# Two-layer hybrid encoder trunk on one core: the projections' [tokens, columns] copies turned by VectorE squares and tile-to-tile DMAs instead of TensorE transposes

## The chip, the core and the metric

The kernel runs on one core of a Trainium2 chip. The metric is the device time of one execution in microseconds, as a median of repeated runs. The profile comes from one execution of the same program under the hardware profiler.

## What is computed

The reference runs two layers of a mixer over 256 tokens of width 2048 in float32. Cut to what matters:

```python
h = rmsnorm(x, pre_norm_g[l])
proj = jnp.einsum('bsd,dn->bsn', h, w_in[l])
(qa, ka, va, qb, kb, vb, qc, kc, vc, za, zb, zc, gates) = jnp.split(proj, split_points, axis=-1)
ya = neighbourhood_attention(heads(qa, 8), heads(ka, 8), heads(va, 8), rpb[l])
yb = gqa_attention(axial_rope(rmsnorm(qb)), axial_rope(rmsnorm(kb)), vb)
yc = dilated_mixture(heads(qc, 12), heads(kc, 12), heads(vc, 12))
merged = sum(g_i * einsum(y_i * silu(z_i), w_branch_i) for the branches a, b, c)
x = x + rmsnorm(einsum(merged, w_out[l]), post_norm_g[l])
```

The scores need q and k with the head's 128 columns on the partitions and tokens along the free axis, and the branch products need silu(z) times the attention output in the same layout. The projections leave PSUM with tokens on the partitions. Turning them from [tokens, columns] to [columns, tokens] is the work this case is about.

## The kernel before

All weights stream once through the core. The unit is a chunk: 256 rows by 512 columns of a weight matrix (512 KB, tile `raw`). ScalarE casts it to a rounded high part `wh` (L171), VectorE subtracts to get the low part `wl` (L176), and TensorE multiplies both token tiles T = 0, 1 (128 tokens each) with it in three passes per 128 rows (high by high, low by high, high by low; L146 to L148). That is 12 matmuls of 512 columns a chunk. A projection block (512 output columns) has 8 chunks; a layer has 23 projection blocks for q, k, v and z, then four rounds of gates and branch products, then four output blocks.

The order is written out by hand and each engine runs its own list in order. For each chunk `ahead` issues the load of the chunk 6 later on SyncE's queue (SP), the cast of the chunk 3 later and the subtraction of the chunk 2 later; after the chunk's matmuls `slot()` adds a little of the other work. `slot()` takes up to two steps of the evacuation queue `evq`, one step of every job that has started (`active`), and then starts one waiting job: a light one from `light`, once its slot has passed, or, if `light` is empty, an attention head from `heavy`.

An evacuation of a q, k or z block copies PSUM to the tile `tok` (ScalarE, L299 or L325, the z blocks with a VectorE step at L326; the branch B blocks with the rotation at L483 to L493), first for T = 0 and a slot later for T = 1. Each then calls `later(tr_job(...))`. `tr_job` (L280) is the code that changes. For one token tile it makes four TensorE transposes against the identity into the PSUM tile `tp` (L284), and then either splits `tp` into a high part (ScalarE, L130) and a low part (VectorE, L132), or, for the operands that are used unsplit, copies it (ScalarE, L289). A layer has 17 blocks of four 128-column heads and one (the keys of branch B) of two, so 36 blocks in the program and 280 transposes. Of the 18 blocks of a layer 9 are split (q and k of branch A and of group 0 of branch C, q and k of branch B) and 9 are copied (five z blocks, q and k of groups 1 and 2 of branch C).

Nearly every tile lives in one pool `up` of 47 buffers of 4 KB a partition (helper `U`): weights before and after the split, `tok`, the attention operands and the probabilities. A load waits on SP until the buffer that it gets has been released.

The attention jobs (`head_job`, `job_c`) also use TensorE transposes, of the probabilities (L140, L380). These stay.

Of the kernel before, what the change touches and what calls it, by code (L numbers as in the profile page):

```python
# [10 lines left out]
F32 = mybir.dt.float32  # L11
# [9 lines left out]
P = 128  # L21
# [6 lines left out]
LA_RAW, LA_HI, LA_LO = 6, 3, 2  # L28
LAG = 6


class Blk:
    """One 512-column block of a projection: K chunks of 256 rows, both token tiles."""

# [13 lines left out]
def trunk(ctx, tc, x, xT, wpack, wbr_a, wbr_b, wbr_c, wout, pre_g, qk_g, bgate, post_g, abias,  # L48
# [31 lines left out]
    nc.gpsimd.memset(mhalf, -0.5)  # L80
    # the engines wake while the first loads are under way
    nc.scalar.activation(mhalf[:, 0:1], mhalf[:, 0:1], AF.Copy)
# [5 lines left out]

# [1 line left out]
    evq, light, heavy, active = deque(), deque(), deque(), []  # L90
    flow = dict(cool=0, hold=True, slot=0, split=9)

    def later(g, wait=0):
        """a filler for a following slot, once what it needs is under way"""
        light.append((flow["slot"] + wait, g))
# [24 lines left out]

# [1 line left out]
    def rsqrt(v, n):  # L122
        """1/sqrt of a small positive f32 tile"""
        y = small.tile([P, n], F32, name="rs_y")
        nc.gpsimd.tensor_tensor(out=y, in0=v, in1=mhalf[:, :n], op=ALU.pow)
        return y

    def split(src, h, lo, scale=1.0):
        """src * scale -> h + lo, both exactly representable for the one-pass products."""
        nc.scalar.activation(h, src, AF.Copy, scale=scale)  # L130
        if isinstance(scale, float) and scale == 1.0:
            nc.vector.tensor_tensor(out=lo, in0=src, in1=f32(h), op=ALU.subtract)  # L132
        else:
            nc.vector.scalar_tensor_tensor(lo, src, scale, f32(h), op0=ALU.mult, op1=ALU.subtract)

    def four_T(src):
        """Four [128,128] transposes side by side in one bank."""
        tp = aux.tile([P, 4, P], F32, name="tp", bufs=2)
        for j in range(4):
            nc.tensor.transpose(tp[:, j, :], src(j), ident)  # L140
        return tp

    def mm3(out_, lhs, rhs, first, last):
        """out_ += lhs.T @ rhs for (high, low) pairs: one-pass products"""
        (lh, ll), (rh, rl) = lhs, rhs
        nc.tensor.matmul(out_, lhsT=lh, rhs=rh, start=first, stop=False)  # L146
        nc.tensor.matmul(out_, lhsT=lh, rhs=rl, start=False, stop=False)  # L147
        nc.tensor.matmul(out_, lhsT=ll, rhs=rh, start=False, stop=last)  # L148

# [1 line left out]
    stream = []  # L151
# [51 lines left out]

# [1 line left out]
    prev = {}  # L205

    def layer(l):
# [5 lines left out]

        # -- the layer's input: hT = (x * gain) transposed, 1/rms kept apart --
        def sq_step(nb, T):
# [23 lines left out]
        def ht_x(nb, js):  # L239
            """from the host's transposed layout of x"""  # L240
            t = S["xT", nb]
            if nb not in HT:
                HT[nb] = pair("hT", [4, 256])
            for j in js:
                split(t[:, j], HT[nb][0][:, j], HT[nb][1][:, j], scale=gain(nb * 4 + j))

        def ht_psum(nb, T):
            """from the previous layer's output: residual, transposes"""
            if nb not in HT:
                HT[nb] = pair("hT", [4, 256])  # L250
            h, lo = HT[nb]
            tp = four_T(lambda j: X[nb][:, T, j * P:(j + 1) * P])
            c = slice(T * P, (T + 1) * P)
            t = work.tile([P, 4, P], F32, name="s", bufs=2)
            g = gpre[:, l * 16 + nb * 4:l * 16 + nb * 4 + 4]
            for j in range(4):
                nc.scalar.activation(t[:, j], tp[:, j], AF.Copy, scale=g[:, j:j + 1])
            split(t, h[:, :, c], lo[:, :, c])
# [19 lines left out]

        # -- evacuations, per token tile --
        def tr_job(dst, tok, T, n=4):  # L280
            """token-major [tok, n x 128] -> dst[column, block, tokens of T]; a pair is split"""
            tp = aux.tile([P, 4, P], F32, name="tp", bufs=2)
            for j in range(n):
                nc.tensor.transpose(tp[:, j, :], tok[:, T, j * P:(j + 1) * P], ident)  # L284
            c = slice(T * P, (T + 1) * P)
            if isinstance(dst, tuple):
                split(tp[:, 0:n], dst[0][:, 0:n, c], dst[1][:, 0:n, c])
            else:
                nc.scalar.copy(dst[:, 0:n, c], tp[:, 0:n])  # L289
            yield  # L290

        def evac_qk(store, key, which, two):
            tok = {}

            def f(T, ps):
                if T == 0:
                    tok[0] = U("tok", [2, 512])
                    store[key] = pair("qk", [4, 256]) if two else U("qkT", [4, 256])
                nc.scalar.activation(tok[0][:, T], ps, AF.Copy, scale=S[which][T])  # L299
                later(tr_job(store[key], tok[0], T))  # L300
                yield
            return f
# [14 lines left out]
        def evac_z(key):  # L317
            tok = {}

            def f(T, ps):  # L320
                if T == 0:
                    tok[0] = U("tok", [2, 512])
                    SZ[key] = U("z", [4, 256])
                z = tok[0][:, T]
                nc.scalar.activation(z, ps, AF.Tanh, scale=S["rsh"][T])  # L325
                nc.vector.scalar_tensor_tensor(z, z, 1.0, ps, op0=ALU.add, op1=ALU.mult)  # L326
                later(tr_job(SZ[key], tok[0], T), 1)
                yield
            return f

        # -- attention --
        def softmax(sc, p, n, w, f=None):
            """n x w logits a row: exp(f * (s - max)), and the sums"""
            nm = small.tile([P, n], F32, name="nm")
# [10 lines left out]
        def norm(p, sm, n, rsh):  # L345
            """rows divided by their sums, times the gate's factor of the token"""
            r = small.tile([P, n], F32, name="rsum")
# [12 lines left out]
        def head_job(zb, hh, q, k, v, bias=None, f=None):  # L360
            """one head over all 256 keys, both token tiles: q, k give (high, low) of [d, tokens],
            v those of [keys of a tile, d]"""
            sc = aux.tile([P, 2, 256], F32, name="sc")
# [43 lines left out]
        def job_c(hh, dist):  # L407
            """one merged head: the three groups' keys under one softmax"""
            q, k = [QT["c", g] for g in range(3)], [KT["c", g] for g in range(3)]
# [39 lines left out]

        # -- branch A: two units of four heads --  # L450
        def a_unit(u):
# [15 lines left out]

        # -- branch B --
        def b_tables():
# [9 lines left out]
        def rope(dst, ps, T, n, which):  # L479
            """dst = rotation of ps (n heads), the norm's gain in the tables; in two steps"""  # L480
            tb = S["rope"]
# [14 lines left out]
        def head_norm(ps, T, n):  # L496
            """1/rms of each head (of the normalised input's projection)"""
            ss = small.tile([P, n], F32, name="hss")
# [7 lines left out]
        def evac_qb(u):  # L506
            tok = {}

            def f(T, ps):
# [6 lines left out]
                nc.vector.tensor_scalar(S["bf", u][:, :, T], y, S["rss"][T], None, op0=ALU.mult)  # L516
                later(tr_job(QT["b", u], tok[0], T), 1)
                if T == 1:
                    for hh in range(4):
                        heavy.append((2, job_b(u, hh)))  # L520
            return f

        def evac_kvb(T, ps):
# [11 lines left out]
            for i in range(2):  # L535
                t = tok[:, T, i * P:(i + 1) * P]
                nc.scalar.activation(t, t, AF.Copy, scale=f[:, i:i + 1])
            later(tr_job(KT["b"], tok, T, n=2), 1)

# [5 lines left out]

        # -- gates and branch products --
        def merge(nb):
# [44 lines left out]

        # -- output projection, post norm, residual --
        OG, PG, R3 = {}, {}, {}
# [40 lines left out]

        # -- the order of the layer's blocks --
        first = proj(22, evac_z(("c", 0)))
# [56 lines left out]

# [1 line left out]
    nc.sync.dma_start(out=gpre, in_=pre_g)  # L696
# [60 lines left out]
def _tokens():  # L757
    """[2, 128]: the tokens of each tile, t = 4 i + 2 T + s at row 64 s + i"""
    T, s, i = np.meshgrid(np.arange(2), np.arange(2), np.arange(64), indexing="ij")
    return (4 * i + 2 * T + s).reshape(2, P)  # L760
# [27 lines left out]
def _bias_index():  # L788
    """[2, 128, 256] indices into a head's flat (15 x 31) table, 465 where masked"""
    tok = _tokens()  # L790
# [9 lines left out]
def _pack(w):  # L800
    """[L, K, N] -> [L, N/512, K/256, 128, 2*512]"""
    L, K, N = w.shape
# [49 lines left out]
```

## Time and profile before

| | |
|---|---|
| median of 3 runs | 2075.34 us (2074.78 to 2075.48) |
| profiled execution, first to last instruction (span) | 2073.5 us; no other time of that execution is listed |
| TensorE (PE) busy | 2061.9 us, 99% of the span |
| VectorE (DVE) busy | 1163.2 us, 56% |
| ScalarE (ACT) busy | 951.4 us, 46% |
| mean granted TensorE clock | 0.999 |
| bytes moved by DMA | 397.81 MB, 192 GB/s over the span |

PE stands for TensorE's matmuls, PEld for its weight loads, SPq for the issuing of DMAs on SyncE's queue. Matmuls overlap in the pipeline: a matmul is shown with 390 ns, but one starts every 0.23 us, so what an instruction costs on PE is read from the distance between starts, not from its duration.

### The profile page before, as it was taken

How to read it: one execution, taken by the hardware profiler on the slowest of the kernel's cores; microseconds unless marked ns; L12 is line 12 of the kernel's file. 1: busy time of each engine (PE TensorE's matmuls, PEld its weight loads, DVE VectorE, ACT ScalarE, POOL GpSimd, SP SyncE). 2: the span in 40 equal slices, each digit the busy share in tenths (PEclk: the TensorE clock that was granted, in tenths of full speed). 3: DMA queues.
4: the chain of work that ended last, by engine and by line, in shares of the span. 5: the costliest groups of instructions: out<-in, count | busy, mean ns of one | idle time of the engine just before them, and what ended most of it. 6: DMA issues, size and time to landing. Idle time of an engine off the chain costs nothing.

```text
span 2073.5 us, 24944 instructions
## 1 busy us (share of the span) xinstructions
PE 2061.9 (99%) x9634; PEld 1716.2 (83%) x9634; DVE 1163.2 (56%) x1445; ACT 951.4 (46%) x1370; POOL 23.2 (1%) x31
## 2 busy tenths in 40 slices
PE   9999999999999999999999999999999999999998
PEld 7888888888888888888888888888888888888886
DVE  6444466565776554645554445565657764646454
ACT  6443354444554434443564444454445543443332
POOL 0000000000000000000000000000000000000000
PEclk9999999999999999999999999999999999999999
DMA  9555455645546655667565554555454466656662
GB/s 373 190 173 187 153 173 179 213 156 185 168 163 208 203 198 188 203 228 259 174 228 171 188 183 142 182 176 200 164 187 163 168 213 200 197 191 208 228 241 71
DMA packets 115270, 397.81 MB, mean 192 GB/s; under 512 B 12752, under 2 KB 12880, under 8 KB 115152
## 3 DMA queue, kind: packets, MB, share of 16 engines
q1 hardware_dynamic: 115152, 396.23, 56.5%
q8 instruction: 75, 1.23, 0.2%
q14 instruction: 43, 0.35, 0.1%
HBM read 391.99 MB, written 4.19 MB: 191 GB/s over the span
## 4 chain that ended last, share of the span: by engine, by line
PE 99%; DMA 0%; ACT 0%; DVE 0%; SPq 0%; issue 0%; DVEq 0%; POOLq 0%; ACTq 0%
PE acc L148 31%; PE acc L146 31%; PE acc L147 31%; PE tp L284 1%; PE tp L140 1%; PE tp L380 1%; PE o L148 0%; PE sc L148 0%; PE o L147 0%; PE sc L147 0%; PE o L146 0%; PE sc L146 0%; DMA raw<-in_wpack_dram 0%; PE o L446 0%; PE sc L418 0%; DVE x L597 0%
## 5 line engine op out<-in xcount | busy, mean ns | idle before, releaser
L176 DVE TENSOR_TENSOR wl<-raw,wh 128x1024 fp32r<-128x1024 f32 (+1 forms) x706 | 831.7, 1217 | 172.1 <-ACT wh L171 169.3
L146 PE MATMUL acc<-wh,hTh 128*128 128x512 f32 x2240 | 886.3, 396 | 0.6 <-ACT wh L171 0.6
L147 PE MATMUL acc<-wl,hTh 128*128 128x512 f32 x2240 | 873.8, 390 | 0.8 <-DVE wl L176 0.8
L148 PE MATMUL acc<-wh,hTl 128*128 128x512 f32 x2240 | 873.8, 390 | 0.0
L171 ACT CAST wh<-raw 128x1024 fp32r<-128x1024 f32 (+1 forms) x706 | 699.3, 1043 | 40.0 <-DVE wl L176 12.9
L148 PEld LDWEIGHTS acc<-wh,hTl 128*128 128x128 f32 x2240 | 420.6, 188 | 89.0
L147 PEld LDWEIGHTS acc<-wl,hTh 128*128 128x128 f32 x2240 | 421.5, 188 | 84.9 <-DVE wl L176 2.6
L146 PEld LDWEIGHTS acc<-wh,hTh 128*128 128x128 f32 x2240 | 421.2, 188 | 83.3 <-ACT wh L171 1.6
L564 ACT ACTIVATE g<-g 128x512 f32<-128x512 f32 x48 | 30.4, 633 | 232.8 <-DVE g L563 232.8
L563 DVE SCALAR_TENSOR_TENSOR g<-acc,rsx,bg 128x512 f32<-128x512 f32 x48 | 35.9, 747 | 173.6 <-PE acc L148 173.6
L146 PE MATMUL acc<-wh,yTh 128*128 128x512 f32 x320 | 124.5, 389 | 0.0
L147 PE MATMUL acc<-wl,yTh 128*128 128x512 f32 x320 | 124.5, 389 | 0.0
L148 PE MATMUL acc<-wh,yTl 128*128 128x512 f32 x320 | 124.5, 389 | 0.0
L146 PE MATMUL acc<-wh,mTh 128*128 128x512 f32 x256 | 100.4, 392 | 0.0
L148 PE MATMUL acc<-wh,mTl 128*128 128x512 f32 x256 | 99.7, 390 | 0.0
L147 PE MATMUL acc<-wl,mTh 128*128 128x512 f32 x256 | 99.7, 389 | 0.0
L299 ACT ACTIVATE tok<-acc,rsx 128x512 f32<-128x512 f32 x40 | 27.6, 689 | 124.9 <-PE acc L148 124.9
L340 ACT ACTIVATE sp<-sp,nm 128x256 f32<-128x256 f32 (+1 forms) x48 | 27.6, 577 | 109.4 <-DVE nm L335 109.4
L579 DVE SCALAR_TENSOR_TENSOR g<-g,acc 128x512 f32<-128x512 f32 x48 | 32.8, 683 | 78.6 <-PE acc L148 78.6
L147 PEld LDWEIGHTS acc<-wl,yTh 128*128 128x128 f32 x320 | 60.1, 188 | 12.5
L146 PEld LDWEIGHTS acc<-wh,yTh 128*128 128x128 f32 x320 | 60.1, 188 | 12.5
L130 ACT ACTIVATE mTh<-tp 128x512 fp32r<-128x512 f32 x16 | 9.6, 598 | 132.4 <-PE tp L140 132.4
(116 smaller groups left out, 1172.2 us busy)
## 6 DMA issues: line engine op xcount, KB each, us to landing
raw<-in_wpack_dram SPq DMA_DIRECT2D x558, 512.0 KB, 3.5
raw<-in_wo_dram SPq DMA_DIRECT2D x64, 512.0 KB, 5.2
raw<-in_wa_dram SPq DMA_DIRECT2D x32, 512.0 KB, 3.3
raw<-in_wb_dram SPq DMA_DIRECT2D x32, 512.0 KB, 3.7
raw<-in_wc_dram SPq DMA_DIRECT2D x16, 512.0 KB, 3.8
bg<-in_bgate_dram SPq DMA_DIRECT2D x24, 256.0 KB, 3.8
x<-in_x_dram SPq DMA_DIRECT2D x8, 512.0 KB, 7.9
abias<-in_abias_dram SPq DMA_DIRECT2D x8, 512.0 KB, 4.2
```

Source lines behind the costliest of these rows:

```text
L140: nc.tensor.transpose(tp[:, j, :], src(j), ident)
L146: nc.tensor.matmul(out_, lhsT=lh, rhs=rh, start=first, stop=False)
L147: nc.tensor.matmul(out_, lhsT=lh, rhs=rl, start=False, stop=False)
L148: nc.tensor.matmul(out_, lhsT=ll, rhs=rh, start=False, stop=last)
L171: nc.scalar.copy(HI[i][:, k], RAW[i][:, k])
L176: nc.vector.tensor_tensor(out=LO[i][:, k], in0=RAW[i][:, k], in1=f32(HI[i][:, k]), op=ALU.subtract)
L284: nc.tensor.transpose(tp[:, j, :], tok[:, T, j * P:(j + 1) * P], ident)
L299: nc.scalar.activation(tok[0][:, T], ps, AF.Copy, scale=S[which][T])
L340: nc.scalar.activation(p[:, i], sc[:, i], AF.Exp, bias=nm[:, i:i + 1], scale=1.0 if f is None else f[:, i:i + 1], accum_out=sm[:, i:i + 1])
L563: nc.vector.scalar_tensor_tensor(g, ps, S["rs"][T], BG[i], op0=ALU.mult, op1=ALU.add)
L564: nc.scalar.activation(g, g, AF.Tanh, scale=0.5)
L579: nc.vector.scalar_tensor_tensor(G[i][:, T], G[i][:, T], 1.0, ps, op0=ALU.add, op1=ALU.mult)
```

## The change

The transposes at L284 go. One `tr_job` now serves both token tiles of a block; it starts after the T = 1 evacuation. VectorE turns each of the two [128 x 512] halves of `tok` in squares of 32 x 32 into a new tile `tt` (one instruction for each half, STREAM_TRANSPOSE). The squares then stand turned in themselves but in the wrong partitions. Sixteen DMAs on SP, each of 32 partitions by 256 floats (32 KB; 16 KB for the two-head block), carry square row i, column j to partitions 32 j of a second new tile `tx`. The job then lets three slots pass (`TR_WAIT`), and the split or copy reads `tx` in SBUF where it read `tp` in PSUM. The heads of branch B are queued when the job of their q block has ended, where before they were queued with its last evacuation.

```diff
+TR_WAIT = 3
...
-        def tr_job(dst, tok, T, n=4):
-            tp = aux.tile([P, 4, P], F32, name="tp", bufs=2)
-            for j in range(n):
-                nc.tensor.transpose(tp[:, j, :], tok[:, T, j * P:(j + 1) * P], ident)
-            c = slice(T * P, (T + 1) * P)
-            if isinstance(dst, tuple):
-                split(tp[:, 0:n], dst[0][:, 0:n, c], dst[1][:, 0:n, c])
-            else:
-                nc.scalar.copy(dst[:, 0:n, c], tp[:, 0:n])
-            yield
+        def tr_job(dst, tok, n=4, then=None):
+            tt, tx = U("tt", [4, 2, n * 32]), U("tx", [4, 2, n * 32])
+            for T in range(2):
+                nc.vector.transpose(out=tt[:, :, T].rearrange("p j (h a) -> p h j a", h=n), in_=tok[:, T])
+            for i in range(4):
+                for j in range(4):
+                    nc.sync.dma_start(out=tx[j * 32:(j + 1) * 32, i], in_=tt[i * 32:(i + 1) * 32, j])
+            for _ in range(TR_WAIT):
+                yield
+            for T in range(2):
+                src = tx[:, :, T].rearrange("p i (h a) -> p h i a", h=n)
+                v = lambda t: t[:, 0:n, T * P:(T + 1) * P].rearrange("p h (i a) -> p h i a", i=4)
+                if isinstance(dst, tuple):
+                    split(src, v(dst[0]), v(dst[1]))
+                else:
+                    nc.scalar.copy(v(dst), src)
+            if then:
+                then()
...
-                later(tr_job(store[key], tok[0], T))
+                if T == 1:
+                    later(tr_job(store[key], tok[0]))
...
-                later(tr_job(SZ[key], tok[0], T), 1)
+                if T == 1:
+                    later(tr_job(SZ[key], tok[0]), 1)
...
-                later(tr_job(QT["b", u], tok[0], T), 1)
                 if T == 1:
-                    for hh in range(4):
-                        heavy.append((2, job_b(u, hh)))
+                    later(tr_job(QT["b", u], tok[0],
+                                 then=lambda: heavy.extend((2, job_b(u, hh)) for hh in range(4))), 1)
...
-            later(tr_job(KT["b"], tok, T, n=2), 1)
+            if T == 1:
+                later(tr_job(KT["b"], tok, n=2), 1)
```

The two places below show how the instructions of the engines now stand.

SP, from the first loads of layer 0 to past its third z block. Before, the weight loads follow each other; the only other rows are the distance and bias tables:

```order
L711 DMA rope_c<-in_rope_dram 128x512
L165 DMA raw<-in_wpack_dram 128x1024 x74
L542 DMA dist<-in_dist_dram 128x1024
L165 DMA raw<-in_wpack_dram 128x1024 x17
L457 DMA abias<-in_abias_dram 128x1024 x2
```

Now, the same place:

```order
L723 DMA rope_c<-in_rope_dram 128x512
L166 DMA raw<-in_wpack_dram 128x1024 x10
L289 DMA tx<-tt 32x256 x16
L166 DMA raw<-in_wpack_dram 128x1024
L289 DMA tx<-tt 32x256 x16
L166 DMA raw<-in_wpack_dram 128x1024 x8
L289 DMA tx<-tt 32x256 x16
L166 DMA raw<-in_wpack_dram 128x1024 x8
L289 DMA tx<-tt 32x256 x16
L166 DMA raw<-in_wpack_dram 128x1024 x8
```

Sixteen small transfers now stand in the row of weight loads for every turned block, eight loads apart where turned blocks follow each other; the first two groups are one load apart. The blocks of v have none.

ScalarE, a copied block (q of group 1 of branch C). Before:

```order
L299 ACTIVATE tok<-acc,rsx 128x512
L171 CAST wh<-raw 128x1024
L299 ACTIVATE tok<-acc,rsx 128x512
L289 COPY qkT<-tp 128x4x128
L171 CAST wh<-raw 128x1024
L289 COPY qkT<-tp 128x4x128
L171 CAST wh<-raw 128x1024 x6
```

Now:

```order
L309 ACTIVATE tok<-acc,rsx 128x512
L172 CAST wh<-raw 128x1024
L309 ACTIVATE tok<-acc,rsx 128x512
L172 CAST wh<-raw 128x1024 x4
L298 COPY qkT<-tx 128x4x128 x2
L172 CAST wh<-raw 128x1024 x3
```

The copies moved from the slots of the evacuation to four weight casts behind it, and stand together.

VectorE, a split block (q of group 0 of branch C, the second block of the layer). Before:

```order
L326 SCALAR_TENSOR_TENSOR tok<-tok,acc 128x512
L176 TENSOR_TENSOR wl<-raw,wh 128x1024 x3
L132 TENSOR_TENSOR qkl<-tp,qkh 128x4x128
L176 TENSOR_TENSOR wl<-raw,wh 128x1024
L132 TENSOR_TENSOR qkl<-tp,qkh 128x4x128
```

Now, with the z block's job before it:

```order
L337 SCALAR_TENSOR_TENSOR tok<-tok,acc 128x512
L177 TENSOR_TENSOR wl<-raw,wh 128x1024 x2
L286 STREAM_TRANSPOSE tt<-tok 128x4x4x32 x2
L177 TENSOR_TENSOR wl<-raw,wh 128x1024
L286 STREAM_TRANSPOSE tt<-tok 128x4x4x32 x2
L177 TENSOR_TENSOR wl<-raw,wh 128x1024 x3
L133 TENSOR_TENSOR qkl<-tx,qkh 128x4x128 x2
```

The low-part subtractions stand together, behind the turns of their own block and three weight subtractions.

## Rows read from the trace of the kernel before

**Rows 1.** The page: busy times, granted clock, and the chain that ended last.

```profile
PE 2061.9 (99%) x9634; PEld 1716.2 (83%) x9634; DVE 1163.2 (56%) x1445; ACT 951.4 (46%) x1370; POOL 23.2 (1%) x31
...
PE acc L148 31%; PE acc L146 31%; PE acc L147 31%; PE tp L284 1%; PE tp L140 1%; PE tp L380 1%; PE o L148 0%; PE sc L148 0%; PE o L147 0%; PE sc L147 0%; PE o L146 0%; PE sc L146 0%; DMA raw<-in_wpack_dram 0%; PE o L446 0%; PE sc L418 0%; DVE x L597 0%
```

**Rows 2.** Groups of instructions (busy us, mean ns | idle before): PE.

```profile
L284 PE MATMUL tp<-ident,tok 128*128 128x128 f32 x280 | 42.2, 272 | 0.0
```

**Rows 3.** Timeline (start us, us): PE around four transposes.

```profile
78.36 0.39 PE L148 MATMUL acc<-wh,hTl 128*128 128x512 f32 x1
78.59 0.60 PE L284 MATMUL tp<-ident,tok 128*128 128x128 f32 x4
78.94 0.48 PE L146 MATMUL acc<-wh,hTh 128*128 128x512 f32 x1
79.26 0.39 PE L147 MATMUL acc<-wl,hTh 128*128 128x512 f32 x1
```

**Rows 4.** Groups of DVE and ACT: the nearest shapes to the new instructions.

```profile
L351 DVE TENSOR_SCALAR sp<-sp,rsum 128x512 f32<-128x512 f32 x16 | 7.8, 488 | 0.6
L493 DVE TENSOR_TENSOR tok<-tok,s 128x512 f32<-128x512 f32 x8 | 5.5, 692 | 0.3
L176 DVE TENSOR_TENSOR wl<-raw,wh 128x1024 fp32r<-128x1024 f32 x702 | 829.1, 1220 | 171.6 <-ACT wh L171 168.9 <-DMA raw<-in_wpack_dram 2.6
L564 ACT ACTIVATE g<-g 128x512 f32<-128x512 f32 x48 | 30.4, 633 | 232.8 <-DVE g L563 232.8
L171 ACT CAST wh<-raw 128x1024 fp32r<-128x1024 f32 x702 | 696.9, 1045 | 39.5 <-DVE wl L176 12.9 <-PE acc L147 12.4 <-DMA raw<-in_wpack_dram 7.2
```

**Rows 5.** Timeline of ACT, then DVE, at the third block's end (last: idle before).

```profile
74.70 0.69 ACT L299 ACTIVATE tok<-acc,rsx 128x512 f32<-128x512 f32 x1 [6.94 <-PE acc L148]
75.29 1.04 ACT L171 CAST wh<-raw 128x1024 fp32r<-128x1024 f32 x1
76.23 0.69 ACT L299 ACTIVATE tok<-acc,rsx 128x512 f32<-128x512 f32 x1
...
76.36 1.23 DVE L176 TENSOR_TENSOR wl<-raw,wh 128x1024 fp32r<-128x1024 f32 x1 [5.80 <-ACT wh L171]
```

**Rows 6.** Timeline of SP: early loads, a wait-free pair, and loads of layer 0.

```profile
18.40 0.33 SPq L165 DMA_DIRECT2D raw<-in_wpack_dram  x1
19.68 0.38 SPq L73 DMA_DIRECT2D x<-in_x_dram  x1
...
26.96 42.82 SPq L165 DMA_DIRECT2D raw<-in_wpack_dram  x24
...
633.32 0.33 SPq L165 DMA_DIRECT2D raw<-in_wb_dram  x1
633.69 0.43 SPq L553 DMA_DIRECT2D bg<-in_bgate_dram  x1
```

**Rows 7.** The page: DMA queue (packets, MB, share); issues (KB each, us to landing).

```profile
q1 hardware_dynamic: 115152, 396.23, 56.5%
...
raw<-in_wpack_dram SPq DMA_DIRECT2D x558, 512.0 KB, 3.5
...
out_dram<-x SPq DMA_DIRECT2D x8, 256.0 KB, 2.8
...
gpre<-in_pre_g_dram SPq DMA_DIRECT2D x1, 16.0 KB, 1.8
```

**Rows 8.** SP's waits (us in total, times, longest).

```profile
SPq L165 <- PE acc L148: 734.6, 254, 7.1
...
SPq L165 <- DMA raw<-in_wpack_dram: 10.5, 13, 0.9
```

**Rows 9.** Timeline of DVE, then of ACT, among heads of branch C.

```profile
271.93 0.42 DVE L355 TENSOR_TENSOR z<-o,z 128x256 f32<-128x256 f32 x1 [2.84 <-PE o L446]
...
278.09 1.99 ACT L171 CAST wh<-raw 128x1024 fp32r<-128x1024 f32 x2
283.65 0.73 ACT L340 ACTIVATE sp<-sp,nm 128x512 f32<-128x512 f32 x1 [3.58 <-DVE nm L335]
```

## Prediction, written before the result was known

> **What bounds the kernel now.** I read the page first. PE is busy 99% of the span and the chain that ended last names PE in all its large shares [rows 1]; its two other large users, DVE at 56% and ACT at 46% [rows 1], have room on average. So time falls by what is taken off PE's list, unless the new work makes PE wait. The groups by line give the count of what is taken off: 280 transposes at L284 [rows 2], and the chain gives them a share of 1% [rows 1]. Then I read distances between starts on PE, since durations overlap, and last the timelines of ACT, DVE and SP around a turned block, because the question is what is late next there.
>
> **What goes from PE.** Undisturbed, a matmul starts 0.23 us after the one before (L148 at 78.36, the next instruction at 78.59). Across four transposes L148 to L147 takes 79.26 - 78.36 = 0.90 us instead of two steps, 0.453 us [rows 3]. So four transposes cost 0.447 us. The 280 are 68 groups of four and 4 groups of two: 68 x 0.447 + 4 x 0.224 = 31.3 us. PE waits for nothing in front of L284 (idle 0.0) [rows 2], so no hidden wait goes with them. The attention's transposes at L140 and L380 stay.
>
> **What DVE and ACT get.** 72 turns (68 of 128x512). The trace has no 32 x 32 turn; a one-input instruction of 128x512 takes 0.488 us, a two-input one 0.692, one of twice the columns 1.220 [rows 4]. I take 0.69, the slower of the two of the same size, and keep 0.49 and 1.22 as ends: 50 us in all (35 to 88). DVE goes from 1163 to some 1213 us of 2044, 59%. Nothing of that is on the path as long as `wl` stays ahead of PE. The splits and copies keep their number; they read SBUF where they read PSUM, about 0.63 us for ACT by the nearest row from SBUF [rows 4].
>
> **What SP gets, and who waits.** 576 transfers of 32 KB (16 KB in the two-head blocks), 16 a job. Issuing costs the distance of two starts: 0.37 us where nothing held it (633.32 to 633.69) [rows 6]. I take 0.38 each, so 16 hold SP for 6 us in a block that lasts 8 chunks, 8 x 12 x 0.227 = 21.8 us; with eight loads at 0.38 SP is then used 9 of 21.8 us. The upper end is 1.28 us, the step between early loads (18.40, 19.68), when the engines of the DMA were full [rows 6]. Landing of a 32 KB tile-to-tile transfer is not in the trace: 1.8 us for 16 KB, 2.8 for a 256 KB store from SBUF, 3.5 for a weight load [rows 7]. I take 2.8, a transfer that also starts in SBUF, with 1.8 and 3.5 as ends.
>
> Behind the transfers on SP stand the weight loads. They are far ahead: the 24 loads that began from 26.96 to 69.8 us [rows 6] are chunks 13 to 36 (13 more went out in the start-up lines). PE begins chunk 24 at 75.9, as worked out below, so chunk 36 twelve chunks later, at 108.5: 39 us after its issue. Much of SP's list waits for buffers that PE has to release (734.6 us on one line alone) [rows 8], so SP is early, not busy. That also means that SP will stand at the first transfer of a job, waiting for DVE's turn, with later loads held behind it. The first load that it holds is the one that `ahead` issues in the following slot.
>
> **Clock of one job.** Let t0 be PE's start on the next block. The third block: the T = 0 transposes stand behind 12 matmuls of the next block, so t0 = 78.59 - 2.72 = 75.87 [rows 3]. `tok` of T = 1 is written from 76.23 to 76.92 and DVE's next `wl` ends at 77.6 [rows 5]; the two turns follow, to t0 + 3.1. Sixteen issues: the last at 3.1 + 15 x 0.38 = t0 + 8.8, landed at t0 + 11.6. The job's last part comes three slots after its first, in slot 5 after the block's last chunk, which PE ends at t0 + 13.6. Before it ACT has cast up to 8 chunks ahead of t0 and DVE subtracted up to 7.
>
> - *Split job* (18 of 36): from the landing two casts at 0.63, one low part at 0.69 and `wl` at 1.22 [rows 4], 3.2 us, must end when PE needs that `wl`, at 7 x 2.72 + 0.23 = t0 + 19.3. So the landing may be as late as t0 + 16.1: 4.5 us to spare.
> - *Copy job* (the other 18): two copies, a weight cast at 1.05 and `wl`, 3.5 us, by t0 + 22.0: landing by t0 + 18.5.
> - *The held load*: issued at t0 + 9.2, landed 3.5 later, cast and subtracted by t0 + 15.0; needed at t0 + 22.0.
>
> Among heads the picture is the same with PE setting the pace. After the first z block of branch A the turns stand behind `z<-o` at 271.93 [rows 9]: turned at 273.7, last issue at 279.4, landed at 282.2. In ACT's list the copy stands between the casts that ended at 280.1 and an exp that started at 283.65 because it had to wait for scores [rows 9]. The copies are done at 283.4. They fill an existing wait.
>
> The heads of a q block of branch B start about two slots later than before; their product is used 30 chunks behind the block, some 80 us, so that costs nothing. The 18.3 MB more of DMA are under 5% of the 397.81 MB.
>
> **Sum.** The profiled span is 2073.5 us, 1.8 under the median of the runs; I take that difference as unchanged. 2075.3 - 31.3 = 2044.0 us, 1.5% faster. A measurement of this kernel can tell about 0.2% (4 us) from no change.
>
> **A rule that speaks against it.** The rows show that transfers overlap: eight or so early DMAs were under way at steps of 1.28 us while a load takes 3.5 us to land [rows 6, 7]. The Trainium skill, "DMA: Bandwidth & Descriptors", section "Rules for kernel authors", says to join many small transfers into one large one, since under 64 KB one pays mostly overhead. The transfers here have half that. Taken at its strongest, each would pay its fixed part alone; from rows, 16 times the 1.8 us of the smallest transfer [rows 7]. Then the landing is at 3.1 + 15 x 1.8 + 1.8 = t0 + 31.9, 15.8 us late for a split job and 13.4 for a copy, 526 us in all: 2570 us. The overlap in the rows speaks against it: 0.02.
>
> The same skill, "VectorE: DVE Perf Modes", section "Rules for kernel authors", advises TensorE for a 128 x 128 transpose when PSUM will do as its target. By its times one operation would be the measure; here the row says that PE is the engine that is full [rows 1], and the sum goes by that.
>
> **Rivals.**
>
> *Part of the gain is lost in waits.* Transfers start every 0.67 us (half of the step of the early loads) and land after 3.5: landing at 3.1 + 10.0 + 3.5 = t0 + 16.6, 0.5 us late for a split job; 18 x 0.5 = 9 us, 2053 us. For it: SP does wait for older DMAs to land at times (13 times, 0.9 us at the longest) [rows 8]. Against: 0.37 us between starts where nothing held. 0.13.
>
> *Slower: the transfers come too slowly and hold ACT, DVE and the loads behind them.* At a step s the landing is t0 + 5.9 + 15 s; split jobs are late from s = 0.68, and from 0.80 on (18 x (15 s - 10.2) = 31.3 us) the whole gain is spent. At the early step of 1.28 and a landing of 3.5 us it is t0 + 25.8: 9.7 us late for 18 jobs, 7.3 for 18, 306 us in all, 2350 us. For it: loads and transfers share one queue, and that queue's packets take 56.5% of the DMA engines' time already [rows 7]. Against: SP stands before each job for several us, so that older loads have landed. 0.09, with the rule's case above 0.11.
>
> *The transposes were free.* If PE's list only looks full and the next limit is close behind (weight splitting on DVE, say), the time stays at 2075. Against: PE never waited at L284 and DVE is at 59% with the new work. 0.04.
>
> **How the numbers follow.** The forecast as worked out, from 2040 to 2050, has 0.72. The first rival fills 2050 to 2071. With the two sides of no change and slower cut off (0.15) and the upper part of the first rival too, 2039 to 2058 holds about 0.8. Faster: 0.72 + 0.13 = 0.85; same: 0.04; slower: 0.11.
>
> **What would show it.** In the profile after: L284 gone, PE's instructions 280 fewer, PE still 99% and its busy time about 31 us shorter; turns of 0.5 to 0.7 us; steps of 0.38 us between the starts of the sixteen transfers and landings of 2 to 3 us; waits of ACT for `tx` in place of those for `tp`, and next to none of PE for `wh` or `wl`. If PE waits for `wh` or `wl` grow by more than some 10 us in all, the forecast is wrong; if they stand behind waits of ACT for `tx`, the transfers are slow, and if behind waits for `raw`, the held loads are.

## The result, and the profile after

| | before | after |
|---|---|---|
| median of the runs (4 each) | 2075.06 us | 2138.53 us |
| lowest and highest | 2074.34 to 2075.48 | 2135.98 to 2138.92 |
| ratio, 95% interval | | 1.0303 [1.0288, 1.0317] |
| profiled execution: span | 2073.5 us | 2136.8 us |
| mean granted TensorE clock | 0.999 | 0.985 |

The change makes the kernel 3.0% slower; 2044.0 us (2039 to 2058) was predicted. It took the road of the rival "Slower", and at a step of some 0.67 us between the transfers, at which the prediction's own clock still gave 2053.

The page of the changed kernel (busy us, share of the span, instructions; then the chain that ended last; then DMA issues with KB each and median us to landing) answers to [rows 1, 7]:

```profile
PE 2062.4 (97%) x9354; PEld 1700.6 (80%) x9354; DVE 1207.0 (56%) x1517; ACT 961.5 (45%) x1370; POOL 23.3 (1%) x31
...
PE 58%; SPq 5%; DMA 3%; DVE 3%; ACT 2%; issue 1%; ACTq 0%; DVEq 0%; POOLq 0%
...
raw<-in_wpack_dram SPq DMA_DIRECT2D x558, 512.0 KB, 5.2
...
tx<-tt SPq DMA_DIRECT2D x544, 32.0 KB, 1.9
```

PE has its 280 instructions less, and yet as much busy time as before (2061.9). That is the first thing to see: 31 us of work went, and as much came back as longer busy time of the matmuls that are left. PE idles 2136.8 - 2062.4 = 74.4 us, before 2073.5 - 2061.9 = 11.6. SP, which had 0% in the chain, now has 5% of the span (the chain is followed back to 591.9 us only), and a weight load takes 5.2 us to land instead of 3.5.

The waits of the changed kernel (us in total, times, longest) name who stands where; those of PE for weights, the last two, are 48.2 us and were 1.4 us in all before:

```profile
ACT qkh L131 <- DMA tx<-tt: 137.3, 16, 12.4
...
ACT wh L172 <- DMA raw<-in_wpack_dram: 90.9, 109, 4.9
...
ACT qkT L298 <- DMA tx<-tt: 75.7, 8, 10.4
...
ACT z L298 <- DMA tx<-tt: 66.5, 9, 11.2
...
PE acc L148 <- DVE wl L177: 42.7, 29, 6.8
...
PE acc L147 <- ACT wh L172: 5.5, 8, 1.1
```

ACT stands for `tx` (280 us in these three rows) *and* for `raw` (91 us). The prediction had said that the one would show slow transfers and the other held loads; both are there. The tile `tx`, and the turns, have these durations (ns, least/median/most):

```profile
L289 SPq DMA_DIRECT2D tx<-tt x576: 507/589/1894, 51.2 to 1674.1; - x192
L286 DVE STREAM_TRANSPOSE tt<-tok x72: 401/672/707, 49.9 to 1663.9; 128x512 f32<-128x512 f32 x68, 128x256 f32<-128x256 f32 x4
```

A turn takes 0.67 us, as forecast (0.69). An issue takes 0.59 us of SP, not 0.38. Where that leads is in the timelines of SP, ACT and DVE for one round, from one job's transfers to the next (start us, us; in brackets the idle time before and its releaser):

```profile
63.35 10.32 SPq L289 DMA_DIRECT2D tx<-tt  x16
73.77 4.10 SPq L166 DMA_DIRECT2D raw<-in_wpack_dram  x8
85.58 11.20 SPq L289 DMA_DIRECT2D tx<-tt  x16
96.89 4.08 SPq L166 DMA_DIRECT2D raw<-in_wpack_dram  x8
108.16 4.31 SPq L289 DMA_DIRECT2D tx<-tt  x7
```

```profile
74.98 1.15 ACT L131 ACTIVATE qkh<-tx 128x512 fp32r<-128x512 f32 x2 [7.50 <-DMA tx<-tt]
...
98.23 1.14 ACT L298 COPY qkT<-tx 128x512 f32<-128x512 f32 x2 [10.36 <-DMA tx<-tt]
100.45 1.05 ACT L172 CAST wh<-raw 128x1024 fp32r<-128x1024 f32 x1 [1.07 <-DMA raw<-in_wpack_dram]
...
104.58 1.04 ACT L172 CAST wh<-raw 128x1024 fp32r<-128x1024 f32 x1
```

```profile
105.66 1.23 DVE L177 TENSOR_TENSOR wl<-raw,wh 128x1024 fp32r<-128x1024 f32 x1 [0.30 <-ACT wh L172]
106.80 1.30 DVE L286 STREAM_TRANSPOSE tt<-tok 128x512 f32<-128x512 f32 x2
```

Read it as a ring. The sixteen transfers hold SP from 85.58 to 96.78. The weight loads behind them go out from 96.89; the first is cast at 100.45, the fourth at 104.58, its `wl` is formed from 105.66 to 106.89. Only then, in DVE's list, comes the next block's turn, and 0.06 us after its end the next transfers start. One round takes 108.16 - 85.58 = 22.58 us, while PE needs 21.76 for the block's eight chunks; the next three, to 131.15, 152.49 and 175.15, take 22.99, 21.34 and 22.66 us. SP is not early, as the prediction had it: it goes round with ACT and DVE, and mostly slower than PE.

In this stretch the ring costs PE nothing yet: PE stood until 78.13, runs behind since, and doesn't wait again before 298.57. In layer 1 the chain that ended last goes round the ring itself, from one job's transfers (from 1167.28) to the next (from 1189.70), 22.42 us (start us, us):

```profile
1178.01 4.20 DMA raw<-in_wpack_dram
1182.24 1.06 ACT wh L172
...
1186.13 1.04 ACT wh L172
...
1187.20 0.65 DVE wl L177
...
1188.97 0.68 DVE tt L286
```

From there it goes on over these transfers, their landing, the split and a `wl` to a wait of PE of 1.21 us, at 1204.61.

Beside the ring, the copy at 98.23 waited 10.36 us for its transfers, and the split of the first q block 7.50 us until 74.98. That split is where PE loses most at once. Its timeline (matmuls of 0.23 us a step until 70.90) and the window of that stretch (length, busy us of PE, PEld, DVE, ACT, POOL, then the granted clock, the DMA share and GB/s):

```profile
70.90 0.39 PE L147 MATMUL acc<-wh,hTh 128*128 128x512 f32 x1
78.13 0.80 PE L148 MATMUL acc<-wl,hTh 128*128 128x512 f32 x1 [6.84 <-DVE wl L177]
...
79.14 0.63 PE L147 MATMUL acc<-wh,hTh 128*128 128x512 f32 x1
79.57 0.63 PE L148 MATMUL acc<-wl,hTh 128*128 128x512 f32 x1
```

```profile
73.60:83.40 9.80, 5.27 (x12) 4.18 (x13) 6.42 (x7) 5.99 (x8) 0.00 (x0) 0.50 0.89 331
```

After the gap the granted clock is 0.50, the lower of the two levels (1.2 of 2.4 GHz), and the steps between matmuls are 0.43 us (79.14 to 79.57) instead of 0.23 [rows 3]. Eleven such stretches come, the first the longest (10.2 us), each with gaps of PE before it. Where no block is turned almost nothing is lost: from 620 to 1000 us PE is busy 378.06 of 380.00 us, and the rest is one wait of a head of branch B at 622.31.

### The profile page after: what moved, and what is told of

Its sections match the earlier page's. It is cut to its first block, busy times and chain, and to the rows that moved or that the text cites. A ratio compares the mean times of both kernels' runs of the same rounds, so it can differ in the third digit from the quotient of the medians.

```text
span 2136.8 us, 25336 instructions
## 1 busy us (share of the span) xinstructions
PE 2062.4 (97%) x9354; PEld 1700.6 (80%) x9354; DVE 1207.0 (56%) x1517; ACT 961.5 (45%) x1370; POOL 23.3 (1%) x31
## 4 chain that ended last, share of the span: by engine, by line
PE 58%; SPq 5%; DMA 3%; DVE 3%; ACT 2%; issue 1%; ACTq 0%; DVEq 0%; POOLq 0%
PE acc L148 19%; PE acc L149 18%; PE acc L147 18%; SPq L289 5%; DMA raw<-in_wpack_dram 2%; DVE wl L177 1%; DMA tx<-tt 1%; ACT wh L172 1%; PE tp L141 1%; DVE tt L286 1%; PE tp L392 0%; DVE qkl L133 0%; PE o L148 0%; PE sc L149 0%; PE o L149 0%
## 5 line engine op out<-in xcount | busy, mean ns | idle before, releaser
L148 PE MATMUL acc<-wl,hTh 128*128 128x512 f32 x2240 | 884.2, 395 | 42.8 <-DVE wl L177 42.7
L172 ACT CAST wh<-raw 128x1024 fp32r<-128x1024 f32 (+1 forms) x706 | 708.4, 1045 | 127.4 <-DMA raw<-in_wpack_dram 90.9
L148 PEld LDWEIGHTS acc<-wl,hTh 128*128 128x128 f32 x2240 | 426.1, 190 | 139.9 <-DVE wl L177 55.1
L147 PEld LDWEIGHTS acc<-wh,hTh 128*128 128x128 f32 x2240 | 425.7, 190 | 94.9 <-ACT wh L172 9.3
L149 PEld LDWEIGHTS acc<-wh,hTl 128*128 128x128 f32 x2240 | 425.5, 190 | 89.6
L133 DVE TENSOR_TENSOR qkl<-tx,qkh 128x512 fp32r<-128x512 f32 x32 | 20.7, 689 | 138.8 <-ACT qkh L131 138.8
L131 ACT ACTIVATE qkh<-tx 128x512 fp32r<-128x512 f32 x32 | 18.5, 624 | 137.3 <-DMA tx<-tt 137.3
L149 PEld LDWEIGHTS acc<-wh,yTl 128*128 128x128 f32 x320 | 60.1, 188 | 12.5
```

Of the source, the lines that this page charges most:

```text
L172: nc.scalar.copy(HI[i][:, k], RAW[i][:, k])
```

## The experiments

Two theories stood at first. **Landing**: the transfers land later than the three slots allow, ACT and DVE stand at the split or copy with weights queued behind. **Hold**: sixteen issues hold SP so long that the weight loads come late. Neither was enough alone, as the first two runs show.

**The job waits six slots.** Edit of the changed kernel:

```diff
-TR_WAIT = 3
+TR_WAIT = 6
```

> The changed kernel with TR_WAIT 6 in place of 3: ACT and DVE come to the split or copy three slots (8 us) later; the sixteen transfers and their place on SP are the same. Theory L (ACT and DVE stand too early at the landing of tx, and wl is queued behind them) expects nearly all of PE's 63 us of new idle time gone, the granted clock at 1.0 throughout, and 2044 to 2060 us. Theory H (SP is held about 11 us a job by issuing, and the weight loads behind it land too late) expects the waits of ACT for raw (91 us in the changed kernel) to stay or grow and 2100 to 2140 us.

Measured: 2154.32 us against 2075.33, 1.038 [1.0359, 1.04], slower still than with three slots. The waits of ACT for `tx` are gone from the top of the list, and others have come:

```profile
ACT wh L172 <- DMA raw<-in_wpack_dram: 388.7, 91, 15.6
...
PE acc L148 <- DVE wl L177: 39.1, 32, 4.3
...
PE acc L147 <- ACT wh L172: 25.7, 17, 4.0
```

A longer margin for the landing alone doesn't help. SP's timeline says why: a round is now 136.89 - 111.99 = 24.9 us.

```profile
111.99 10.68 SPq L289 DMA_DIRECT2D tx<-tt  x16
...
136.89 5.59 SPq L289 DMA_DIRECT2D tx<-tt  x9
```

The late copy of the job before (1.13 us, at 132.28 on ACT) now stands among the casts that lie ahead of the next turn, and lengthens the ring. In this stretch PE waits in every round for a `wh` or a `wl`, for 1.00 us at 127.24 and 1.33 us at 151.66.

**The hold alone.** The kernel before, which keeps its transposes; beside them sixteen transfers a block that nobody reads, from `tok`:

```diff
+            if T == 1:
+                tx = U("tx", [4, 2, n * 32])
+                for i in range(4):
+                    for j in range(4):
+                        nc.sync.dma_start(out=tx[j * 32:(j + 1) * 32, i],
+                                          in_=tok[i * 32:(i + 1) * 32].rearrange("p t n -> p (t n)")[:, j * n * 64:(j + 1) * n * 64])
```

> The kernel before, TensorE transposes and all, with sixteen 32 KB transfers a block from tok to a tile that nobody reads, issued on SP at the T = 1 transposes. It does more than the reference needs and leaves nothing out. Only SP is held; ACT and DVE wait for no transfer. Theory H expects PE waits behind late loads and a time 20 to 80 us over the kernel before, 2095 to 2155 us. Theory L expects at most 5 us more, 2075 to 2080 us.

Measured: 2075.94 us against 2075.33, 1.0005 [0.9995, 1.0015]: no difference, though SP is held exactly as long and ACT waits for loads more than in the changed kernel:

```profile
75.55 11.20 SPq L294 DMA_DIRECT2D tx<-tok  x16
...
97.41 11.21 SPq L294 DMA_DIRECT2D tx<-tok  x16
```

```profile
ACT wh L171 <- DMA raw<-in_wpack_dram: 138.4, 72, 8.5
```

The theory of the hold alone falls. Here the transfers wait for `tok`, which is written at the evacuation, not for a turn that stands behind further `wl` on DVE, and nothing waits for them; PE's block is also some 0.9 us longer, with its eight transposes still in it. So the hold needs something beside it: the way back to SP, the ring, or an ACT that has waited for `tx` before it comes to the held loads. The ring is the next theory, beside the landing.

**Issued by GpSimd, six slots.**

```diff
-TR_WAIT = 3
+TR_WAIT = 6
...
-                    nc.sync.dma_start(out=tx[j * 32:(j + 1) * 32, i], in_=tt[i * 32:(i + 1) * 32, j])
+                    nc.gpsimd.dma_start(out=tx[j * 32:(j + 1) * 32, i], in_=tt[i * 32:(i + 1) * 32, j])
```

> The changed kernel with the sixteen transfers issued by GpSimd, which is idle 99% of the time, and TR_WAIT 6. SP has weight loads alone again. Theory H expects 2044 to 2055 us if GpSimd issues one transfer in at most 1 us, with ACT waiting for raw as little as in the kernel before (under 10 us). Theory L expects the same time as e1. If GpSimd takes over 1.4 us for each, tx lands after slot 8 and the waits for tx come back, 2080 us and more.

Measured: 2044.15 us, 0.9848 [0.9832, 0.9865]. With the ring cut and the margin long the forecast of 2044.0 is met. PE's busy time is 2061.9 - 2028.7 = 33.2 us less, within 2 us of the predicted sum:

```profile
PE 2028.7 (99%) x9354; PEld 1687.7 (83%) x9354; DVE 1202.5 (59%) x1517; ACT 948.3 (46%) x1370; POOL 306.8 (15%) x607
```

**Through DRAM.** Five DMAs a job on SP instead of sixteen; three slots as in the change:

```diff
             for i in range(4):
-                for j in range(4):
-                    nc.sync.dma_start(out=tx[j * 32:(j + 1) * 32, i], in_=tt[i * 32:(i + 1) * 32, j])
+                d = scr[st["job"]].rearrange("(j q) (i c) -> q j i c", q=32, c=1024 // 4)[:, :, i, :n * 64]
+                nc.sync.dma_start(out=d, in_=tt[i * 32:(i + 1) * 32].rearrange("p j t c -> p j (t c)"))
+            nc.sync.dma_start(out=tx.rearrange("p i t c -> p i (t c)"),
+                              in_=scr[st["job"]].rearrange("p (i c) -> p i c", i=4)[:, :, :n * 64])
```

> The changed kernel with the squares carried through a DRAM tensor: four stores of 32 partitions by 4 KB a job and one load of 512 KB, five DMAs on SP in place of sixteen, TR_WAIT 3. The load waits on SP until the stores have landed. Hold of SP some 0.6 x 4 + 3 + 0.4 = 6 us in place of 11, tx complete some 9 us behind the turn in place of 13. Both theories expect fewer stalls; with both waits below their limits 2044 to 2055 us. If the stores' landing takes over 6 us, no better than the changed kernel.

Measured: 2047.16 us, 0.9867 [0.9853, 0.9882]. The same data by a longer way, in fewer issues, is fast even with three slots. So the turns as such cost nothing. Fewer issues shorten the hold and the way to the landing together, so this run doesn't tell which of the two counts. PE waits 3.2 us for the `qkh` of two heads of branch B, which is what is left of the landing.

The next two runs take away the held loads and leave the margin as it is.

**Loads nine chunks ahead instead of six.** A load's `wl` is formed two chunks ahead of its use. With loads issued six ahead, four chunks lie between a load and its `wl`, and so of the eight loads behind a job the first four have their `wl` ahead of the next turn. With nine, only the first has.

```diff
-LA_RAW, LA_HI, LA_LO = 6, 3, 2
+LA_RAW, LA_HI, LA_LO = 9, 3, 2
```

> The changed kernel with weight loads issued 9 chunks ahead in place of 6. Hold of SP, TR_WAIT and the distance from turn to landing are as in the changed kernel; only the load that the next block's turn has to wait for is now the first behind the transfers and no longer the fourth. Theory R (a loop: sixteen issues hold SP 11 us, the loads behind land 3.6 us later and 1.35 us apart, the turn of the next block stands on DVE behind the wl of the fourth of them, and the next transfers behind that turn; 22.5 us or more around against 21.8 us of PE work in a block) expects about 18.5 us around, groups of transfers 21.8 us apart in the blocks without heads, nearly no PE waits and 2044 to 2065 us. Theory M (each job by itself lands too late, 13 us behind its turn, for what ACT and DVE have in hand among heads) expects the PE waits among heads to stay and 2095 to 2135 us.

Measured: 2105.98 us against 2075.49, 1.0149 [1.0134, 1.0165]. The waits for `raw` shrink from 90.9 us to 8.0, those of the splits for `tx` stay:

```profile
ACT qkh L131 <- DMA tx<-tt: 152.4, 16, 14.0
...
PE acc L148 <- DVE wl L177: 29.1, 17, 6.5
```

Half of the loss is gone (32.5 of 63.5 us), and with it the waits for the loads that were held. Not all of it need be the ring's: among heads the changed kernel also waits for held loads where the ring isn't closed. There ACT had stood for `tx` until 316.90, and then came to a load that had gone out behind the transfers:

```profile
322.75 1.04 ACT L172 CAST wh<-raw 128x1024 fp32r<-128x1024 f32 x1 [4.69 <-DMA raw<-in_wpack_dram]
```

PE waited 2.85 us for the `wl` of this load, until 327.20, although the block's turn, at 302.95, had stood behind a head's work and not behind a held load. What stays in the run with nine are the waits for the landing.

**Issued by GpSimd, three slots.** The edit is that of the run with six, without `TR_WAIT`.

> The changed kernel with the transfers issued by GpSimd and TR_WAIT 3 as in the changed kernel, so that the landing is as late as there (some 10 us of issuing and 3.8 us to land) and only SP is free. Theory R expects 2044 to 2055 us, the same as with TR_WAIT 6. Theory M expects the waits of ACT for tx and of PE behind them to stay, 2090 us and more.

Measured: 2139.55 us, 1.0316 [1.0298, 1.0333], as slow as the change itself, with ACT's wait for `raw` at 7.9 us. The landing alone can cost as much as both: on this queue a transfer takes 3.5 us to land instead of 1.9, and the splits wait longer in all than in any other run.

```profile
ACT qkh L131 <- DMA tx<-tt: 159.5, 16, 14.0
...
tx<-tt POOLq DMA_DIRECT2D x544, 32.0 KB, 3.5
```

**Half on SP, half on GpSimd, three slots.**

```diff
-                    nc.sync.dma_start(out=tx[j * 32:(j + 1) * 32, i], in_=tt[i * 32:(i + 1) * 32, j])
+                    (nc.sync if i < 2 else nc.gpsimd).dma_start(out=tx[j * 32:(j + 1) * 32, i], in_=tt[i * 32:(i + 1) * 32, j])
```

> The changed kernel with eight of a job's sixteen transfers on SP and eight on GpSimd, TR_WAIT 3. SP is held about 5.5 us a job. Theory R: 17 us around, 2044 to 2050 us. Theory M: tx complete some 8 us behind the turn, 2044 to 2060 us too. Both at once; it shows the time at half the hold.

Measured: 2055.88 us, 0.9908 [0.9893, 0.9922]. Eight issues on each side shorten hold and landing together, and 82.7 us of the changed kernel's time go. Of PE's 11.5 us of waits 7.1 are for `qkh` of two heads. The Trainium skill, "DMA: Bandwidth & Descriptors", section "Issuing engines are not separate DMA queues", says that issuing on several engines saves only the sequencer's time to initiate a DMA, usually small beside the DMA. The landing agrees (1.9 us beside 0.59 for one issue); with sixteen in a row the measurement decides otherwise, since 10 to 11 us of issuing is the larger part.

**What an issue costs, by its ends.** The kernel before with transfers that nobody reads, one shape a block: 32 partitions of 256 floats to other partitions (`ya`), 128 of 64 (`yb`), 32 of 256 to the same partitions (`yc`), the latter to DRAM (`scr_dram`), and four of 128 by 256 (`ye`).

```diff
+                if k == 0:
+                    ya = U("ya", [4, 256])
+                    for i in range(4):
+                        for j in range(4):
+                            nc.sync.dma_start(out=ya[j * 32:(j + 1) * 32, i], in_=src[i * 32:(i + 1) * 32, j * 256:(j + 1) * 256])
+                elif k == 1:
+                    yb = U("yb", [16, 64])
+                    for i in range(16):
+                        nc.sync.dma_start(out=yb[:, i], in_=src[:, i * 64:(i + 1) * 64])
...
+                elif k == 3:
+                    for i in range(4):
+                        for j in range(4):
+                            nc.sync.dma_start(out=scr[st["job"], i * 32:(i + 1) * 32, j * 256:(j + 1) * 256],
+                                              in_=src[i * 32:(i + 1) * 32, j * 256:(j + 1) * 256])
```

> The kernel before with transfers on SP that nobody reads, one shape a block in turn: sixteen of 32 partitions by 256 floats from tok to other partitions, sixteen of 128 partitions by 64 floats, sixteen of 32 by 256 to the same partitions, sixteen of 32 by 256 to DRAM, four of 128 by 256. If the price of issuing hangs on having both ends in SBUF, all but the DRAM ones take 0.5 to 0.6 us on the queue; if on the 32 partitions, the 128-partition ones take 0.33 us and the others 0.5 to 0.6. The time of the kernel is not the question; 2070 to 2080 us.

The tiles of that kernel (ns of an issue on SP, least/median/most; first and last start):

```profile
L298 SPq DMA_DIRECT2D ya<-tok x112: 507/588/1655, 46.2 to 1509.4; - x112
```

```profile
L302 SPq DMA_DIRECT2D yb<-tok x112: 465/599/1242, 58.9 to 1530.0; - x112
```

```profile
L307 SPq DMA_DIRECT2D yc<-tok x112: 507/588/1196, 76.2 to 1580.5; - x112
```

```profile
L316 SPq DMA_DIRECT2D ye<-tok x24: 464/556/602, 120.7 to 1446.8; - x24
```

```profile
L311 SPq DMA_DIRECT2D scr_dram<-tok x112: 302/419/1752, 98.0 to 1605.6; - x112
```

Neither the number of partitions nor their change nor the size sets the price: with both ends in SBUF it is 0.56 to 0.60 us, and 0.42 when the target is DRAM. The time, one run of 2075.51 us, says nothing further.

**Both limits lifted, on SP.**

```diff
-LA_RAW, LA_HI, LA_LO = 6, 3, 2
+LA_RAW, LA_HI, LA_LO = 9, 3, 2
...
-TR_WAIT = 3
+TR_WAIT = 6
```

> The changed kernel with both earlier edits at once: loads 9 chunks ahead and TR_WAIT 6; all sixteen transfers stay on SP at 0.6 us each. Each edit alone left the kernel slower than the one before (2106 and 2154 us). If the changed kernel is slow by two separate limits (R: the loop through the held loads is longer than a block; M: the split or copy comes sooner than tx lands), lifting both gives what lifting them by other means gave, 2044 to 2052 us, with no transfer made cheaper. If the 0.6 us a transfer of SP is what costs in itself, it stays above 2075 us.

Measured: 2042.53 us against 2075.37, 0.9841 [0.9824, 0.9857], faster than both kernels, with every one of the sixteen issues still on SP. PE's waits are down to 2.4 us, 1.5 of them at the start. The page, then SP, then DVE:

```profile
PE 2030.1 (99%) x9354; PEld 1689.0 (83%) x9354; DVE 1204.9 (59%) x1517; ACT 957.6 (47%) x1370; POOL 22.4 (1%) x31
```

```profile
81.09 13.22 SPq L289 DMA_DIRECT2D tx<-tt  x16
...
101.61 13.41 SPq L289 DMA_DIRECT2D tx<-tt  x16
```

```profile
99.14 1.22 DVE L177 TENSOR_TENSOR wl<-raw,wh 128x1024 fp32r<-128x1024 f32 x1 [8.02 <-ACT wh L172]
100.28 1.30 DVE L286 STREAM_TRANSPOSE tt<-tok 128x512 f32<-128x512 f32 x2
```

SP is held 13.2 us here, longer than in the slow kernel, and still a round takes 101.61 - 81.09 = 20.5 us, less than PE's 21.76 (the next three take 20.6, 22.4 and 20.8): one `wl` of a held load stands ahead of the turn, not four. The issues have not become dearer (0.59 us at the median); SP now waits within the groups for older weight loads to land, 24.0 us in all against 5.9 in the changed kernel:

```profile
SPq L289 <- DMA raw<-in_wpack_dram: 24.0, 27, 1.7
```

**Through DRAM, six slots.** The edit of the run through DRAM, and `TR_WAIT = 6`.

> The five-DMA kernel through DRAM with TR_WAIT 6 in place of 3. Theory M says that its last PE waits (heads of branch B waiting for qkh, 4 us in all) are those of a landing that is late by a little, and expects 2043 to 2046 us; if they come from the later start of these heads they stay or grow, 2047 us or more.

Measured: 2044.93 us, 0.9853 [0.9838, 0.9868]. Against three slots that is 2.2 us less, under what a measurement of this kernel can tell, though the wait for `qkh` is gone from PE's list. With five issues a job the margin hardly matters.

The four runs on SP side by side:

| | three slots | six slots |
|---|---|---|
| loads 6 ahead | 2138.5 | 2154.3 |
| loads 9 ahead | 2106.0 | **2042.5** |

Lifting one limit gains 32.5 us or loses 15.8; lifting both gains 96.0.

## Why the prediction was wrong

**The saving was right.** 31.3 us were worked out; with the stalls gone the kernel gains 32.8 us (2075.37 - 2042.53) on SP and 31.2 (2075.33 - 2044.15) on GpSimd. The turns on DVE, at 0.67 us, are hidden as forecast.

**The term that was mis-sized** is the issue price: "I take 0.38 each, so 16 hold SP for 6 us". Measured are 0.59 us an issue and 10.0 to 11.4 us for sixteen in the first stretch of layer 0, 0.63 to 0.71 each. The 0.38 came from a step behind a load from DRAM [rows 6]; the transfers have both ends in SBUF, and that is what costs. The landing, 1.9 us where 2.8 was taken, erred the other way.

**That size alone doesn't give the loss.** With 11.2 us and 1.9 the prediction's formula lands the transfers at 3.1 + 11.2 + 1.9 = t0 + 16.2, a tenth of a microsecond behind its limit for split jobs. The step that failed beside it is the clock of one job itself, in two places:

- *The held load* was followed to PE ("needed at t0 + 22.0"), not to the next turn. Four held loads have their `wl` ahead of that turn, so the hold comes back to its own start: SP, ACT, DVE, SP. Of the 22.58 us of a round 11.2 are the hold; with the 6 us of the forecast and all else as it is the same round would take 17.4 (an estimate from these rows), well inside PE's 21.76. The hold isn't all of it: the next rounds hold SP for 10.0, 10.0 and 10.3 us and take 22.99, 21.34 and 22.66. Shown is that the held loads cost (nine loads ahead gain 32.5 us), that the hold with nothing waiting behind it costs nothing, and that the chain goes round the ring in layer 1. Not shown is how much of the 32.5 us is the closed ring and how much held loads that ACT comes to late, as at 322.75.
- *The margin* was taken for a job by itself. The first two jobs of layer 0 come one load apart: the second one's turn ended at 54.8, its transfers had to wait until 63.35 for the first sixteen, and so its split ran at 74.98. Among heads the copies were to be done at 283.4, before an exp that started at 283.65 [rows 9]. Their turns ended at 275.9, the sixteen transfers held SP until 286.9, and the exp came behind the copies, at 289.47 (the line below). And of the later heads of branch B the prediction said "that costs nothing"; PE waited 8.3 us for their `qkh`, 5.5 us of it at once at 585.31. Six slots remove these waits of PE, once the loads are no longer held.

```profile
288.43 1.14 ACT L298 COPY z<-tx 128x512 f32<-128x512 f32 x2 [6.42 <-DMA tx<-tt]
```

**A term was missing.** In the kernel before PE never waits longer than 1.5 us at once, and the sum had no price for what follows a longer gap. Against the run on GpSimd with six slots, which has the same matmuls, the changed kernel is busy 2062.4 - 2028.7 = 33.7 us longer and idle 74.4 - 14.0 = 60.4 us longer; 33.7 + 60.4 = 94.1 is the difference of the spans (2136.8 - 2042.7). So each microsecond more of standing came with about half a microsecond more of busy time. The lower clock is a part of that: the eleven stretches at 0.50 hold 46.5 us of busy PE, and at steps of 0.43 us instead of 0.23 that makes some 22 us (an estimate from these rows). What the other 12 us are, no row here divides.

**The rivals.** "Slower: the transfers come too slowly and hold ACT, DVE and the loads behind them" had the place right and the break-even wrong (0.80 us; the loss was there at 0.67). The first rival had the step, 0.67 (half of 1.28 is 0.64), and gave 2053; with the loads no longer held, the landing by itself cost 2105.98 - 2042.53 = 63.5 us on SP, not 9. That small transfers would be served one after the other did not come: a transfer lands 1.9 us after its issue while the next goes out after 0.65. That transfers overlap was right, though the "eight or so" don't come out of the rows named for them: landings of 3.5 us at steps of 1.28 make about three. The rule that stands with this case (the Trainium skill, "DMA: Bandwidth & Descriptors", section "Rules for kernel authors": join many small transfers) holds in another way than it was weighed: what is paid per transfer is the issuing engine's time, and with both limits lifted even that cost nothing (2042.53 us). That the transposes were free is refuted by the 32.8 us.

**What stays open.** How the loss divides between ring and landing in the changed kernel has no single answer, since they are not additive (the table). Nor do the runs separate the closed ring from held loads that ACT comes to late, or say why SP waits for older loads within its groups.

## What to carry to other kernels

When work moves to a queue, follow the instructions behind it until they come back: what waits for them, and whether that stands ahead, on its own engine, of the work that feeds the queue. A hold that costs nothing on a line costs on a ring as soon as one round is longer than the pacing engine's. Price an issue by a transfer with the same ends, count the jobs that meet as well as one alone, and test two limits together, since lifting one of them can show nothing or a loss.

## What the runs showed of the hardware

- SP's time for one issue depends on where the ends lie: 0.56 to 0.60 us with both in SBUF, 0.42 from SBUF to DRAM, 0.33 to 0.43 for loads from DRAM [rows 6]. Within SBUF, 32 partitions or 128 and 32 KB or 128 KB make no difference beyond that.
- A 32 KB transfer within SBUF lands 1.9 us after its issue on SP; issued on GpSimd, at 0.50 us each, it took 3.5 us with sixteen in a row and 1.8 with eight.
- The granted clock fell to 0.50 after gaps of PE, eleven times in the changed kernel and for up to 10.2 us; that cost some 22 us (the estimate above) of the 33.7.
